# Transposes of rows in groups of eight with both evictions behind them, other places for the first weights and PSUM banks, and later row steps of the norms, in a one-core decoder layer

## The chip, the cores and the metric

The kernel runs on one core of a Trainium2 chip. The metric is the device time of one execution in microseconds (us); for the kernel before, three runs gave a median of 1337.41 us (1336.19 to 1339.85).

## The reference

One post-norm decoder layer over 1024 rows (time steps) of width 1024, all in fp32:

```
proj = h @ w_in                      # 1024 x 2824, split among three mixers
y    = concat(ssd(...), s5(...), rglru(...))            # 1024 x 1024
h = layer_norm(ALPHA*h + y @ w_out, ln1_g, ln1_b)
q, k, v = h @ wq, mem @ wk, mem @ wv                     # 256 memory rows, 4 heads
h = layer_norm(ALPHA*h + softmax(q k^T / 16) v @ wo, ln2_g, ln2_b)
h = layer_norm(ALPHA*h + square(relu(h @ w1)) @ w2, ln3_g, ln3_b)      # hidden width 4096
layer_norm(x, g, b) = (x - mean) * rsqrt(var + 1e-5) * g + b
```

The change touches what follows the mixers: the product with `w_out` and the four other large products, and the first two norms between them.

## The kernel before

**Stages.** The first 368 us compute the mixers; their result y stands transposed (channels on partitions) in SBUF. The rest is a list of eleven phases: the product with `w_out` (phase 0), with `wq` (1), with `wo` (2), and then four pairs of products with a column group of `w1` and a row group of `w2` (phases 3 to 10). Phases with an even number are called "down" (result in rows, added into the residual `acc`), those with an odd number "up" (result transposed, into the hidden tiles `h`). Attention stands between phases 1 and 2.

**Strassen steps.** Each phase multiplies 1024x1024 by 1024x1024 as 2x2 blocks of 512, by seven products of 512x512 blocks instead of eight (Strassen-Winograd). This text writes (p,s) for step s of phase p: (0,6) is the last step of phase 0, (1,0) the first of phase 1. There are 77 steps. `product` (L1242) issues one step on TensorE: 16 groups of three 128x512 matmuls (line L1255), that is 48, because each fp32 operand is held as a high part (cast to fp32r by ScalarE, L82) and a rest (VectorE, L61), tile `A`, which has one place for even and one for odd steps. Casts and splits go in halves of 128x1024, two of the four k slabs of an operand. Most steps take the groups k by k, so that the second half is first needed by the ninth group; (0,6) and (2,6) take them column by column, and need it from the third group on. A dictionary of hooks in `product` runs further code after the group of a given number.

**What stands around each step.** `prep` (L1155) makes the operands of the next step: the sums of blocks that Winograd's form asks for (`sums`, VectorE, L61) and their splits (`put`). `post` (L1262) evacuates a step's PSUM into `acc` (L79 or L61) or `h`. `load_w` (L1133) fetches a weight block in two 512 KB halves on SP's queue into one of four raw weight tiles `wr`. PSUM has two sets, used by steps in turn. TensorE's order is as written by hand; the order on the other engines is set by a scheduler at build time, which follows the order of the code where nothing else decides.

**The norms between phases.** When phase 0 or 2 finishes a block of `acc`, `measured` (L1298) takes row statistics (BN_STATS, L1302), `rstd` (L1291) joins them (BN_AGGR on VectorE, L1293), adds the epsilon on GpSimd (L1294, by the helper at L74) and raises to the power -1/2 on GpSimd (L1295, L61); `centred` (L1306) forms -mean/std on VectorE (`nmr`, L1311) and applies both on ScalarE (L1312), for four tiles of 128 rows in a block. Then `turn` (L1314) transposes the normed rows on TensorE (L1318), eight transposes of 128x128 for two 128x512 results, and evicts each result from PSUM on ScalarE with gain and bias (L1319) into `Z`, the next phase's input. Four such turns are in the last step of the down phase, (0,6) and (2,6), after groups 4, 6, 11 and 13; they turn the block that was finished first. Four more are in the first step of the up phase, (1,0) and (3,0), after groups 7, 9, 13 and 15; they turn the block finished last. `weighted` (L1336) multiplies normed rows by the gain `px` on VectorE and adds them by an accumulating DMA of GpSimd's queue to a copy of the bias in DRAM (`scr_x`), from where `fetched` (L1341) reads the residual back on SP's queue.

**The start of phase 0.** The mixers' last stores of the attention values (`scr_v`, L931) and the first loads of `w_out` into `wr` (L1141) stand in SP's queue one behind the other. During (0,0) TensorE also transposes the last four tiles of y (L951) and the norms' gains (`columns`).

## Time and profile before

| quantity | value |
|---|---|
| median of 3 runs | 1337.41 us |
| profiled execution, its own time | 1338.34 us |
| span of its trace | 1336.6 us |
| mean granted TensorE clock over the span | 0.975 |
| TensorE busy, share of the span | 95% |
| VectorE, ScalarE, GpSimd busy | 79%, 50%, 16% |

A step without any wait takes 10.9 us, at which 48 matmuls start 0.227 us apart. In the rows of the profile, PE is TensorE, DVE VectorE, ACT ScalarE, POOL GpSimd, SP the sync engine whose queue issues the loads. A row of the timeline gives start, duration, engine, line, operation, output and inputs, and in brackets the idle time before it with the engine that ended it. PEclk is the granted TensorE clock as a share of the full one.

### The profile page before, as it was taken

How to read it: one execution, taken by the hardware profiler on the slowest of the kernel's cores; microseconds unless marked ns; L12 is line 12 of the kernel's file. 1: busy time of each engine (PE TensorE's matmuls, PEld its weight loads, DVE VectorE, ACT ScalarE, POOL GpSimd, SP SyncE). 2: the span in 40 equal slices, each digit the busy share in tenths (PEclk: the TensorE clock that was granted, in tenths of full speed). 3: DMA queues.
4: the chain of work that ended last, by engine and by line, in shares of the span. 5: the costliest groups of instructions: out<-in, count | busy, mean ns of one | idle time of the engine just before them, and what ended most of it. 6: DMA issues, size and time to landing. Idle time of an engine off the chain costs nothing.

```text
span 1336.6 us, 16273 instructions
## 1 busy us (share of the span) xinstructions
PE 1266.8 (95%) x6177; PEld 1058.6 (79%) x6177; DVE 1062.3 (79%) x1431; ACT 669.9 (50%) x875; POOL 216.2 (16%) x219
## 2 busy tenths in 40 slices
PE   7979999998989879999987999999999999999996
PEld 7768777998868668898866888888888888888884
DVE  6959567368889878799777799866987699876987
ACT  6312466455443655484364573355534673355632
POOL 1614343378510210000012000000000000000004
PEclk9989999998999989999988999999999999999998
DMA  6332121345378237003816602512030201212007
GB/s 205 82 92 63 44 57 47 95 140 152 111 277 207 57 66 205 32 17 142 220 34 145 193 23 80 157 48 79 19 99 10 95 32 63 64 39 88 32 0 126
DMA packets 77550, 124.87 MB, mean 93 GB/s; under 512 B 7984, under 2 KB 42784, under 8 KB 77472
## 3 DMA queue, kind: packets, MB, share of 16 engines
q1 hardware_dynamic: 72224, 108.83, 26.3%
q0 software_dynamic: 3312, 12.06, 5.4%
q10 hardware_dynamic: 1936, 2.94, 0.6%
q8 instruction: 48, 0.79, 0.2%
q14 instruction: 30, 0.25, 0.1%
HBM read 106.87 MB, written 29.00 MB: 102 GB/s over the span
## 4 chain that ended last, share of the span: by engine, by line
PE 74%; DVE 5%; DMA 3%; ACT 3%; POOL 2%; issue 2%; SPq 0%; DVEq 0%; POOLq 0%; ACTq 0%
PE P L1255 59%; PE in L87 2%; PE in L89 2%; PE in L88 2%; DMA R<-scr_a 2%; DVE A L61 1%; PE P L1318 1%; DVE bst L1302 1%; POOL bmv L74 1%; DVE acc L61 1%; POOL bmv L61 1%; DVE wr L61 1%; ACT Z L1319 1%; PE sc L87 1%; DMA wr<-in_w_out_dram 1%
## 5 line engine op out<-in xcount | busy, mean ns | idle before, releaser
L1255 PE MATMUL P<-A 128*128 128x512 f32 x3696 | 854.7, 393 | 7.0 <-DVE A L61 3.3
L1255 PEld LDWEIGHTS P<-A 128*128 128x128 f32 x3696 | 699.0, 190 | 153.5 <-DVE A L61 4.1
L82 ACT CAST A<-wr 128x1024 fp32r<-128x1024 f32 x152 | 159.0, 1047 | 123.1 <-PE P L1255 88.5
L61 DVE TENSOR_TENSOR A<-wr,A 128x1024 fp32r<-128x1024 f32 x152 | 184.9, 1219 | 43.8 <-ACT A L82 43.7
L82 ACT CAST A<-h 128x1024 fp32r<-128x1024 f32 x88 | 92.0, 1048 | 169.1 <-PE P L1255 137.0
L74 POOL TENSOR_SCALAR bmv<-bmv 128x1 f32<-128x1 f32 x24 | 13.9, 584 | 851.5 <-DVE bmv L1293 851.5
L61 DVE TENSOR_TENSOR A<-h,A 128x1024 fp32r<-128x1024 f32 x88 | 107.2, 1222 | 42.5 <-ACT A L82 42.5
L61 DVE TENSOR_TENSOR wr<-wr,wr 128x1024 f32<-128x1024 f32 x88 | 106.4, 1220 | 22.9 <-DMA wr<-in_w_dram 19.4
L87 PE MATMUL in<-A,ring 128*128 128x512 f32 x224 | 93.1, 416 | 0.0
L89 PE MATMUL in<-A,ring 128*128 128x512 f32 x224 | 89.6, 400 | 2.3 <-POOL ring L61 2.3
L88 PE MATMUL in<-A,ring 128*128 128x512 f32 x224 | 89.2, 398 | 0.0
L61 POOL TENSOR_TENSOR ring<-raws,ring 128x512 fp32r<-128x512 f32 (+1 forms) x48 | 69.9, 1460 | 103.5 <-ACT ring L82 99.5
L82 ACT CAST A<-Z 128x1024 fp32r<-128x1024 f32 (+1 forms) x53 | 52.9, 1003 | 65.6 <-PE P L1255 52.4
L61 DVE TENSOR_TENSOR acc<-acc,P 128x1024 f32<-128x1024 f32 (+1 forms) x74 | 73.3, 1014 | 6.0 <-PE P L1255 5.3
L82 ACT CAST ring<-raws 128x512 fp32r<-128x512 f32 (+1 forms) x67 | 40.8, 616 | 63.6 <-PE in L88 22.6
L61 DVE TENSOR_TENSOR A<-Z,A 128x1024 fp32r<-128x1024 f32 (+1 forms) x53 | 61.0, 1159 | 13.1 <-ACT A L82 12.7
L89 PEld LDWEIGHTS in<-A,ring 128*128 128x128 f32 x224 | 42.7, 191 | 13.0 <-POOL ring L61 2.8
L87 PEld LDWEIGHTS in<-A,ring 128*128 128x128 f32 x224 | 43.1, 192 | 11.1 <-issue 1.8
L88 PEld LDWEIGHTS in<-A,ring 128*128 128x128 f32 x224 | 42.9, 192 | 10.8 <-issue 1.4
L1318 PE MATMUL P<-ident,acc 128*128 128x128 f32 x128 | 24.0, 312 | 24.4 <-ACT Z L1319 17.3
L1318 PEld LDWEIGHTS P<-ident,acc 128*128 128x128 f32 x128 | 16.8, 156 | 31.7 <-ACT Z L1319 21.4
L1272 ACT COPY h<-P 128x1024 f32<-128x1024 f32 x30 | 30.3, 1013 | 21.9 <-PE P L1255 21.9
(369 smaller groups left out, 1795.8 us busy)
## 6 DMA issues: line engine op xcount, KB each, us to landing
wr<-in_w_dram SPq DMA_DIRECT2D x64, 512.0 KB, 3.6
scr_x<-in_ln_dram SPq DMA_DIRECT2D x16, 512.0 KB, 13.3
scr_x<-acc POOLq DMA_DIRECT2D x16, 512.0 KB, 6.8
acc<-scr_x SPq DMA_DIRECT2D x16, 512.0 KB, 5.5
raws<-in_w_in_dram SPq DMA_DIRECT2D x28, 256.0 KB, 2.9
raws<-in_wk_dram SPq DMA_DIRECT2D x16, 256.0 KB, 3.0
R<-scr_a SPq DMA_DIRECT2D x8, 512.0 KB, 5.3
raws<-in_wv_dram SPq DMA_DIRECT2D x16, 256.0 KB, 2.9
```

Of the source, the lines that this page charges most:

```text
L61: (e or V).tensor_tensor(out=o, in0=a, in1=b, op=op)
L74: (e or V).tensor_scalar(out=o, in0=a, scalar1=s1, scalar2=None, op0=op0)
L82: ins = S.copy(out=hi, in_=src)
L87: PE.matmul(ps, lhsT=l[0], rhs=r[0], start=first, stop=False)
L88: PE.matmul(ps, lhsT=l[0], rhs=r[1], start=False, stop=False)
L89: PE.matmul(ps, lhsT=l[1], rhs=r[0], start=False, stop=last)
L1255: PE.matmul(o, lhsT=l[x_], rhs=r[y_], start=new and k == 0 and m == 0, stop=k == 3 and m == 2, skip_group_check=True)
L1272: S.copy(out=h, in_=p_)
L1302: V.bn_stats(out=st[:, t, d, :], in_=acc[:, t, d * 512:d * 512 + 512])
L1318: PE.transpose(out=ps[:, j * 128:(j + 1) * 128], in_=acc[:, b * 4 + j, k * 128:(k + 1) * 128], identity=ident)
L1319: S.activation(out=X(k // 4 + 1, b)[:, k % 4], in_=ps, func=AF.Identity, scale=lncol[:, 2 * li, k:k + 1], bias=lncol[:, 2 * li + 1, k:k + 1])
```

## The change

It has seven parts:

1. `turn` issues all eight transposes of its two results first and then the two evictions.
2. The turns stand after groups 4, 6, 8 and 10 in (0,6) and (2,6), and after 9, 11, 13 and 15 in (1,0) and (3,0).
3. The hidden tiles get their SBUF place before the raw weight tiles `wr`, and the first `w_out` blocks 11 and 12 go to `wr[0]` and `wr[1]` instead of the other way round.
4. The two PSUM sets of two tiles each are put together from the four tiles in another way.
5. `prep` of step 1 of a phase is split into two parts. At (0,0), (1,0) and (3,0) the first part is emitted ahead of the step's product, and the second part behind it; before, the whole stood behind it.
6. The epsilon is added on VectorE instead of GpSimd.
7. `weighted` is emitted at steps 2 and 3 of phases 1 and 3 instead of steps 1 and 2.

```diff
-    wrp = pool(ctx, "wraw", "right")
-    wr = [wrp.tile([128, 4, 512], F32, name=f"wr{i}") for i in range(4)]
     hp_ = pool(ctx, "hid", "right")
     H = {r: [hp_.tile([128, 4, 512], F32, name=f"h{r}{b}") for b in range(2)] for r in (1, 2)}
+    wrp = pool(ctx, "wraw", "right")
+    wr = [wrp.tile([128, 4, 512], F32, name=f"wr{i}") for i in range(4)]
...
-            PS[:] = [[pl.tile([128, 4 // n, 512], F32, tag=f"P{i}{j}", name="P") for j in range(n)] for i in range(2)]
+            t = [pl.tile([128, 4 // n, 512], F32, tag=f"P{i}", name="P") for i in range(2 * n)]
+            PS[:] = [t[:n], t[n:]] if n == 4 else [[t[3], t[1]], [t[0], t[2]]]
...
-    def prep(i):
+    def prep(i, part=None):
...
-                put(i, 0, W[12])
-                put(i, 1, B(21))
-                sums(W[21], W[21], W[22], ALU.add)
-                sums(W[11], W[21], W[11])
-                sums(sx, B(12), B(11))
-                sums(h_(22), B(22), sx)
+                if part != 2:
+                    put(i, 0, W[12])
+                    put(i, 1, B(21))
+                    sums(W[21], W[21], W[22], ALU.add)
+                    sums(W[11], W[21], W[11])
+                if part != 1:
+                    sums(sx, B(12), B(11))
+                    sums(h_(22), B(22), sx)
...
-                sums(W[21], W[21], W[22], ALU.add)
-                put(i, 0, W[21])
-                sums(sx, B(12), B(11))
-                put(i, 1, sx)
-                sums(W[11], W[21], W[11])
+                if part != 2:
+                    sums(W[21], W[21], W[22], ALU.add)
+                    put(i, 0, W[21])
+                if part != 1:
+                    sums(sx, B(12), B(11))
+                    put(i, 1, sx)
+                    sums(W[11], W[21], W[11])
...
-        ts(mv[:, 1:2], mv[:, 1:2], EPS, ALU.add, e=G)
+        ts(mv[:, 1:2], mv[:, 1:2], EPS, ALU.add)
...
         for n, k in enumerate(ks):
-            ps = P[:, n]
             for j in range(4):
-                PE.transpose(out=ps[:, j * 128:(j + 1) * 128], in_=acc[:, b * 4 + j, k * 128:(k + 1) * 128], identity=ident)
-            S.activation(out=X(k // 4 + 1, b)[:, k % 4], in_=ps, func=AF.Identity, scale=lncol[:, 2 * li, k:k + 1],
+                PE.transpose(out=P[:, n, j * 128:(j + 1) * 128], in_=acc[:, b * 4 + j, k * 128:(k + 1) * 128],
+                             identity=ident)
+        for n, k in enumerate(ks):
+            S.activation(out=X(k // 4 + 1, b)[:, k % 4], in_=P[:, n], func=AF.Identity, scale=lncol[:, 2 * li, k:k + 1],
                          bias=lncol[:, 2 * li + 1, k:k + 1])
...
-    for q, n in ((21, 3), (22, 2), (11, 1), (12, 0)):
+    for q, n in ((21, 3), (22, 2), (11, 0), (12, 1)):
...
+    prep(1, 1)
     product(0, {2: lambda: y_T(4, other[1][:, 0]), 5: lambda: y_T(5, other[0][:, 1]), 8: lambda: y_T(6, other[1][:, 1]),
                 11: lambda: y_T(7, other[0][:, 0]), 15: columns})
-    prep(1)
+    prep(1, 2)
...
-            hooks, late = turns(ph // 2, HB[ph][1], PS[(1 + ph) % 2], (4, 6, 11, 13)), True
+            hooks, late = turns(ph // 2, HB[ph][1], PS[(1 + ph) % 2], (4, 6, 8, 10)), True
...
-            hooks, late = turns(pq // 2, HB[pq][0], PS[(1 + ph) % 2], (7, 9, 13, 15)), True
+            hooks, late = turns(pq // 2, HB[pq][0], PS[(1 + ph) % 2], (9, 11, 13, 15)), True
+            prep(i + 1, 1)
...
-        if ph in (1, 3) and s_ in (1, 2):
-            weighted(ph // 2, HB[ph - 1][2 - s_])
+        if ph in (1, 3) and s_ in (2, 3):
+            weighted(ph // 2, HB[ph - 1][3 - s_])
...
         if late:
-            prep(i + 1)
+            prep(i + 1, 2 if s_ == 0 else None)
```

The lines of the changed kernel are one to eight higher than those of before: the matmuls are at L1260, the transposes at L1322, the evictions at L1325.

What TensorE runs in (0,6) around the four turns, in order; "waits" names the semaphore of the engine that the instruction waits for. Before:

```order
L1318 MATMUL P<-ident,acc 128x128 x4
L1318 MATMUL P<-ident,acc 128x128 [waits Activation_49]
L1318 MATMUL P<-ident,acc 128x128 x3
L1255 MATMUL P<-A 128x512 x6
L1318 MATMUL P<-ident,acc 128x128 [waits DVE_49]
L1318 MATMUL P<-ident,acc 128x128 x3
L1318 MATMUL P<-ident,acc 128x128 [waits Activation_49]
L1318 MATMUL P<-ident,acc 128x128 x3
L1255 MATMUL P<-A 128x512 x15
```

And in the changed kernel:

```order
L1322 MATMUL P<-ident,acc 128x128 x8
L1260 MATMUL P<-A 128x512 x6
L1322 MATMUL P<-ident,acc 128x128 x8
L1260 MATMUL P<-A 128x512 x6
L1322 MATMUL P<-ident,acc 128x128 [waits Activation_49]
L1322 MATMUL P<-ident,acc 128x128 x7
L1260 MATMUL P<-A 128x512 x6
L1322 MATMUL P<-ident,acc 128x128 [waits Activation_49]
L1322 MATMUL P<-ident,acc 128x128 x7
```

The wait between the first and the second four of each turn is gone; the third and the fourth turn wait once each, for evictions of the first and the second.

What VectorE runs from the last row steps of (0,6) into (1,0) (`acc<-acc,P` is the evacuation of (0,6)'s PSUM, `acc<-acc,px` is `weighted`, `A<-` are splits, `wr<-` sums of weights). Before:

```order
L79 SCALAR_TENSOR_TENSOR nmr<-bmv 128x1
L61 TENSOR_TENSOR acc<-acc,px 128x1024 x3
L79 SCALAR_TENSOR_TENSOR acc<-acc,P 128x2x512
L61 TENSOR_TENSOR A<-wr_3506,A 128x1024
L1302 BN_STATS bst<-acc 128x6 x2
L1293 BN_AGGR bmv<-bst 128x2
L61 TENSOR_TENSOR A<-wr_3506,A 128x1024
L79 SCALAR_TENSOR_TENSOR nmr<-bmv 128x1
L1293 BN_AGGR bmv<-bst 128x2
L61 TENSOR_TENSOR A<-Z,A 128x1024
L79 SCALAR_TENSOR_TENSOR nmr<-bmv 128x1
L61 TENSOR_TENSOR A<-Z,A 128x1024
```

And in the changed kernel:

```order
L79 SCALAR_TENSOR_TENSOR acc<-acc,P 128x2x512
L61 TENSOR_TENSOR A<-Z,A 128x1024
L1307 BN_STATS bst<-acc 128x6 x2
L1298 BN_AGGR bmv<-bst 128x2
L61 TENSOR_TENSOR A<-wr_3512,A 128x1024
L74 TENSOR_SCALAR bmv<-bmv 128x1
L1298 BN_AGGR bmv<-bst 128x2
L61 TENSOR_TENSOR A<-wr_3512,A 128x1024
L79 SCALAR_TENSOR_TENSOR nmr<-bmv 128x1
L74 TENSOR_SCALAR bmv<-bmv 128x1
L61 TENSOR_TENSOR A<-Z,A 128x1024
L79 SCALAR_TENSOR_TENSOR nmr<-bmv 128x1
```

`weighted` no longer stands ahead of the evacuation, the epsilon additions (L74) are in VectorE's row, and between the evacuation and the last `nmr` there are four splits of 128x1024 where there were three.

What SP's queue holds at the start of phase 0. Before:

```order
L931 DMA scr_v<-kv 128x256 x2
L1141 DMA wr_3508<-in_w_out_dram 128x2x512
L931 DMA scr_v<-kv 128x256 x2
L1141 DMA wr_3508<-in_w_out_dram 128x2x512
L1141 DMA wr_3507<-in_w_out_dram 128x2x512 x2
L1433 DMA px<-in_ln_dram 48x128
L1141 DMA wr_3506<-in_w_out_dram 128x2x512 x2
```

And in the changed kernel:

```order
L931 DMA scr_v<-kv 128x256 x4
L1142 DMA wr_3515<-in_w_out_dram 128x2x512 x2
L1142 DMA wr_3514<-in_w_out_dram 128x2x512 x2
L1439 DMA px<-in_ln_dram 48x128
L1142 DMA wr_3512<-in_w_out_dram 128x2x512 x2
```

The first half of the first weight block stood ahead of the last two stores and now stands behind them.

More of the change, by code (lines that the diff above doesn't have):

```diff
@@ L1080 @@
     acc = pool(accst, "acc", "left").tile([128, 8, D], F32, name="acc")
+    hp_ = pool(ctx, "hid", "right")
+    H = {r: [hp_.tile([128, 4, 512], F32, name=f"h{r}{b}") for b in range(2)] for r in (1, 2)}
     wrp = pool(ctx, "wraw", "right")
     wr = [wrp.tile([128, 4, 512], F32, name=f"wr{i}") for i in range(4)]
-    hp_ = pool(ctx, "hid", "right")
-    H = {r: [hp_.tile([128, 4, 512], F32, name=f"h{r}{b}") for b in range(2)] for r in (1, 2)}
     PS = []
```

## The prediction

> **What bounds the kernel now.** I read the page first, for the bounding engine:
>
> ```profile
> PE 1266.8 (95%) x6177; PEld 1058.6 (79%) x6177; DVE 1062.3 (79%) x1431; ACT 669.9 (50%) x875; POOL 216.2 (16%) x219
> L1318 PE MATMUL P<-ident,acc 128*128 128x128 f32 x128 | 24.0, 312 | 24.4 <-ACT Z L1319 17.3
> ```
>
> TensorE is busy for 95% of the span, and the largest single idle time that the change touches stands ahead of the norm transposes: 24.4 us, as much as the transposes themselves take. The waits of TensorE split it by what ended it:
>
> ```profile
> PE P L1318 <- ACT Z L1319: 17.3, 16, 3.3
> PE P L1318 <- ACT acc L1312: 7.0, 4, 2.0
> ```
>
> Sixteen waits for the eviction ScalarE makes between the two fours of a turn, and four for normed rows. Then the windows show each step's price. The columns are the stretch, its length, each engine's busy time with its instructions, the granted clock, the DMA share and GB/s. The stretches are the steps (0,6), (1,0), (1,1), (2,6), (3,0), and all steps after 790 us:
>
> ```profile
> 442.30:465.70 23.40, 17.28 (x81) 13.38 (x80) 21.42 (x26) 13.76 (x16) 5.10 (x6) 0.93 0.04 5
> 465.70:492.80 27.10, 19.80 (x81) 15.35 (x81) 17.32 (x20) 14.06 (x16) 4.95 (x6) 0.81 0.41 75
> 492.80:503.70 10.90, 10.90 (x49) 9.01 (x48) 10.90 (x11) 5.22 (x6) 3.46 (x4) 1.00 0.49 73
> 676.00:699.50 23.50, 17.60 (x81) 13.97 (x80) 18.44 (x23) 13.60 (x15) 3.35 (x6) 0.88 0.06 8
> 699.50:724.80 25.30, 18.60 (x82) 14.35 (x81) 17.41 (x20) 13.15 (x15) 4.96 (x6) 0.84 0.69 160
> 790.00:1323.00 533.00, 533.00 (x2354) 441.43 (x2352) 443.16 (x410) 261.32 (x264) 10.14 (x17) 1.00 0.20 61
> ```
>
> An undisturbed step is (1,1): 10.9 us, or 0.227 us for each of 48 matmuls. After 790 us 49 such steps fill 533 us, with TensorE never idle, so nothing can be won there. The four norm steps take 23.4, 27.1, 23.5 and 25.3 us: 99.3 us where four undisturbed ones take 43.6. This is what the change acts on.
>
> **The change part by part. Grouping in eights, later places, in (0,6) and (2,6).** TensorE's timeline in (0,6), at the second four of its first and of its last turn, and at those of the last turn in (2,6) (start, duration, then the idle time before it in brackets):
>
> ```profile
> 446.01 1.19 PE L1255 MATMUL P<-A 128*128 128x512 f32 x4 [1.66 <-DVE A L61]
> 448.51 0.66 PE L1318 MATMUL P<-ident,acc 128*128 128x128 f32 x4 [0.87 <-ACT Z L1319]
> 448.93 1.64 PE L1255 MATMUL P<-A 128*128 128x512 f32 x6
> 461.59 0.87 PE L1318 MATMUL P<-ident,acc 128*128 128x128 f32 x4 [1.85 <-ACT Z L1319]
> 694.75 1.12 PE L1318 MATMUL P<-ident,acc 128*128 128x128 f32 x4 [3.29 <-ACT Z L1319]
> ```
>
> The last four of a turn end and the next matmul starts 448.93-448.51 = 0.42 us behind their start, so eight transposes cost about 0.9 us (an estimate). The 0.87 us wait goes, since the evictions come after the eighth. They need not end before the next matmuls, which write another PSUM set; the third turn needs the first one's tile, two groups of six matmuls (2.7 us) and a turn (0.9 us) later, while two evictions take 1.5 us. The 1.85 and 3.29 us arise because ScalarE runs a norm step ahead of the eviction; in the changed order all evictions of (0,6) stand ahead of the next norm steps. What is late next in (0,6) is the 1.66 us wait for VectorE's split `A`, which no part removes; one more small instruction and a reordered split ahead of it make it about 2.3 (bounds 1.7 and 2.9, one 128x1024 operation more). So (0,6) is 10.9 + 4x0.9 + 2.3 = 16.8, which is 6.6 less than 23.4; the clock, 0.93 before, I put at full, as no gap of TensorE stays over 2.3 us. In (2,6) no split is waited for: 10.9 + 3.6 = 14.5, 9.0 less than 23.5.
>
> **Grouping, later places, the split `prep` and the epsilon, in (1,0) and (3,0).** Here the turns wait for the rows, and VectorE, GpSimd and ScalarE form a chain:
>
> ```profile
> 465.95 1.22 DVE L79 SCALAR_TENSOR_TENSOR acc<-acc,P 128x1024 f32<-128x1024 f32 x1 [0.49 <-PE P L1255]
> 467.09 1.22 DVE L61 TENSOR_TENSOR A<-wr,A 128x1024 fp32r<-128x1024 f32 x1
> 468.22 1.28 DVE L1302 BATCH_NORM_STATS2 bst<-acc 128x6 f32<-128x512 f32 x2
> 469.42 0.19 DVE L1293 BATCH_NORM_AGGREGATE bmv<-bst 128x2 f32<-128x12 f32 x1
> 469.78 1.00 POOL L74 TENSOR_SCALAR bmv<-bmv 128x1 f32<-128x1 f32 x1 [3.17 <-DVE bmv L1293]
> 470.86 0.57 POOL L61 TENSOR_TENSOR bmv<-bmv,nhalf 128x1 f32<-128x1 f32 x1
> 471.47 0.16 DVE L79 SCALAR_TENSOR_TENSOR nmr<-bmv 128x1 f32<-128x1 f32 x1 [0.77 <-POOL bmv L61]
> 473.79 1.24 ACT L1312 ACTIVATE acc<-acc,nmr,bmv 128x1024 f32<-128x1024 f32 x1 [0.89 <-DVE nmr L79]
> ```
>
> A VectorE operation of 128x1024 follows the last after 1.14 us (465.95 to 467.09). Call E the end of (0,6), 465.7 before. The evacuation started at E+0.25 and the last norm step ended at 475.03, E+9.3. The epsilon on GpSimd cost 1.00 us, on VectorE (0.1 us, the step of 469.42) it is cheap, but it now queues behind splits. What of that chain shortens is paid for otherwise: (0,6) is 6.6 us shorter, and VectorE, busy 21.4 of its 23.4 us, has row work left at E. From the last split needed in (0,6), 4.6 us before E, it has 6.0 us of statistics, weight sums and `nmr` to do (three 128x1024, two pairs of statistics, the waits for GpSimd), so the evacuation starts at E+1.5. Then follow the rows of the changed order: evacuation, split, two statistics, split, split at 1.14 each (1.2 for the statistics), small ones 0.3: 6.1 us, and the power, which ends about 0.4 after a VectorE operation that runs beside it:
>
> ```profile
> 1326.14 1.42 DVE L79 SCALAR_TENSOR_TENSOR acc<-acc,bmv,sx 128x512 f32<-128x512 f32 x2
> 1327.06 0.93 POOL L61 TENSOR_TENSOR bmv<-bmv,nhalf 128x1 f32<-128x1 f32 x1
> ```
>
> (1327.99 against 1327.56, where it took 0.93 instead of 0.57). Thus the first `nmr` is at E+8.0; a split, and the power again, the second at E+9.7; its norm step, 1.2 us, ends at E+10.9. The Trainium skill, "GPSIMD Engine Reference", section 1, lists SBUF interfaces shared with VectorE; these two rows agree.
>
> ```profile
> 470.55 0.38 PE L1318 MATMUL P<-ident,acc 128*128 128x128 f32 x2
> 475.09 0.33 PE L1318 MATMUL P<-ident,acc 128*128 128x128 f32 x1 [1.80 <-ACT acc L1312]
> 476.28 1.11 PE L1318 MATMUL P<-ident,acc 128*128 128x128 f32 x4 [0.87 <-ACT Z L1319]
> 477.05 2.91 PE L1255 MATMUL P<-A 128*128 128x512 f32 x6
> ```
>
> Before, TensorE came to its first turn at 470.55 after 21 matmuls, E+4.9. Now it comes after 27, E+6.1, and waits 4.8 us for the last row tile. Behind that stand the turn's last four or five transposes, 0.5, then 21 matmuls, 4.8, and three turns, 2.7: 10.9+8.0 = 18.9, 19.0 rounded, at full clock. At 477.05 six matmuls took 2.91 us instead of 1.64: the clock was at half. The stretches of half clock in these steps, each 3.41 us:
>
> ```profile
> 475.55:478.96 3.41, 2.68 (x9) 2.29 (x10) 3.41 (x4) 2.13 (x3) 0.95 (x1) 0.50 0.41 43
> 478.96:482.37 3.41, 2.54 (x10) 1.84 (x9) 1.65 (x2) 1.15 (x2) 0.00 (x0) 0.50 0.57 111
> 482.37:485.78 3.41, 3.41 (x11) 2.73 (x10) 1.23 (x1) 0.78 (x1) 0.00 (x0) 0.50 0.00 0
> 707.65:711.06 3.41, 1.30 (x6) 1.02 (x6) 3.41 (x4) 1.96 (x2) 1.82 (x2) 0.50 0.69 175
> 711.06:714.47 3.41, 3.41 (x12) 2.61 (x10) 3.31 (x3) 1.82 (x2) 0.00 (x0) 0.50 1.07 174
> ```
>
> TensorE worked 2.68+2.54+3.41 = 8.6 us at half clock in (1,0), a loss of 4.3, and 1.30+3.41 = 4.7 in (3,0), a loss of 2.4. The waits that bring it on stay, so I keep both losses; the bounds are none, and all 8.0 us behind the wait at half clock. (1,0) is 19.0+4.3 = 23.3, 3.8 less than 27.1. In (3,0) a gain multiplication stands in the chain as well; replayed in the same way its last norm step ends at E+12.5, so 12.5+8.0+2.4 = 22.9, 2.4 less than 25.3.
>
> **First weights.** SP's queue at the start, and who waits for it:
>
> ```profile
> 367.11 0.38 SPq L1141 DMA_DIRECT2D wr<-in_w_out_dram  x1
> 368.61 0.80 SPq L931 DMA_DIRECT2D scr_v<-kv  x2
> 386.65 5.52 PE L1255 MATMUL P<-A 128*128 128x512 f32 x16 [1.59 <-DVE A L61]
> ```
>
> The first half block now stands behind the stores that wait until 368.61, and issues near 369.5 instead of 367.11; all weights behind it move too. The sums for (0,1) need the block after it, and TensorE waited for their split at 386.65. I add 1.3 us: between 0 (the loads share the same bandwidth and end no later) and 2.4 (the whole shift).
>
> **Parts at nothing.** The other PSUM tiles only rename what is waited for, and are covered by the 3.6 us between a turn and the next use of its tile. The gain multiplications and their DMAs move to (1,1) to (1,3), where VectorE was full for 10.9 us but TensorE never waited; the splits it needs stand ahead of them. The tail's epsilon changes by under 0.5 us either way, as the power there already runs beside VectorE.
>
> **Sum.** -6.6-9.0-3.8-2.4+1.3 = -20.5, from the profiled execution's 1338.3: 1317.8. The median of the runs shown is 0.9 lower than that execution, so 1317.
>
> **The rivals.** *The clock.* The Trainium skill, "TensorE: Matmul & The Clock Gate", Part 4, says of transposes that the full clock "doesn't engage" for them, because they don't count as busy in the same way. As a mechanism of this kernel: at half clock six matmuls take 2.9 us and eight transposes 1.8 to 2.2, in turns, so no stretch of 3.41 us is filled with matmuls; and 475.55 to 478.96, with 1.9 us of matmuls, did not end the half clock, while 711.06 to 714.47, with some 2.6, did. If it stays down to the end of the turns, (1,0) is 27.0 and (3,0) 28.5, together 9.3 more than my sum: 1326. For: the row of 475.55. Against: that of 711.06. I give 0.22.
>
> *The row chain is no shorter.* GpSimd's power is held up by the splits on VectorE, which now run in denser order, or ScalarE's norm steps queue behind casts; then (1,0) and (3,0) gain nothing: -14.3, 1323. For: (1,0)'s chain is already 1.6 us longer in my replay, relative to E. I give 0.12.
>
> *The chain is freer.* The clock recovers at once and the first weights come no later: 6.7 and 1.3 less, 1309. For: the 1.00 us that an epsilon cost. I give 0.12.
>
> *Slower: SP's queue in phase 3.* With the multiplications a step later, their accumulating DMAs are later, and the reads of `scr_x` that wait for them stand on SP's queue ahead of the second `w2` blocks.
>
> ```profile
> scr_x<-acc POOLq DMA_DIRECT2D x16, 512.0 KB, 6.8
> acc<-scr_x SPq DMA_DIRECT2D x16, 512.0 KB, 5.5
> wr<-in_w_dram SPq DMA_DIRECT2D x64, 512.0 KB, 3.6
> ```
>
> In my replay the weights arrive about 1 us ahead of the sum that (3,4) needs. Each us beyond that costs one, and it decides the sign from 21.5 us of delay on (20.5 and the 1 us), more than one whole pass through the three transfers (15.9); two passes, 31.8 us, would give 1317+31 = 1348. Against: one such pass is what the median transfers take, and they run side by side. I give 0.02. That the change does not do what it says is excluded by the orders: the wait between the fours is gone.
>
> **How the numbers follow.** Forecast 1317, chance 0.5, its own range 1312 to 1321 by the bounds of the split (0.6 each way), the first weights (1.3) and some of the clock. Clock 0.22 at 1326, chain 0.12 at 1323, freer 0.12 at 1309, slower 0.02 at 1348, and 0.02 for several of these losses together, about 1335. The range 1308 to 1327 takes in all but these last two and the tails of the others. 0.3% is 4 us, about what a measurement of this kernel can tell from no change. The slower case lies above that band, and the several losses together reach into it, with a part of the slower case that falls short: faster 0.95, same 0.03, slower 0.02.
>
> **What would show each step.** Right: in the changed profile the idle time ahead of the transposes falls from 24.4 to under 12 us, with no wait for evictions; (0,6) and (2,6) take 16 to 17 and 14 to 15 us; the first turn of (1,0) waits 4 to 6 us for normed rows; half-clock stretches remain in (1,0) and (3,0) only. Wrong: (1,0) or (3,0) above 25 us with a clock below 0.8 would be the clock, above 25 with a late norm step the chain; (0,1) as long as before says that the first weights were not late; a wait for `A` or for `wr` in (1,1) to (3,4) is the queue.

## The result and the profile after

The changed kernel takes 1320.40 us (median of 4 runs, 1319.09 to 1322.26) against 1338.13 us (median of 4) of the kernel before: a ratio of 0.9869, 95% interval 0.985 to 0.9888. The profiled execution took 1319.8 us, with a span of 1318.0. In the profile after, the page's row of busy times:

```profile
PE 1261.5 (96%) x6177; PEld 1057.2 (80%) x6177; DVE 1063.9 (81%) x1455; ACT 667.3 (51%) x875; POOL 216.7 (16%) x195
```

and the norm transposes among the groups of instructions (busy time, mean ns of one, idle time ahead and what ended it):

```profile
L1322 PE MATMUL P<-ident,acc 128*128 128x128 f32 x128 | 20.3, 304 | 9.6 <-ACT acc L1317 9.6
```

The idle time ahead of the transposes fell from 24.4 to 9.6 us. The waits of TensorE say what is left of it, and show two that were not there before:

```profile
PE P L1322 <- ACT acc L1317: 9.6, 4, 3.8
PE P L1445 <- DVE Z L61: 2.2, 1, 2.2
PE P L1260 <- ACT h L1419: 0.7, 1, 0.7
```

No wait for an eviction remains; four waits for normed rows do, two in (1,0) and two in (3,0). The two new ones are the second, ahead of the gains' transpose in (0,0), and the third, in the attention stage. The windows of the changed kernel, in order: (0,0) and (0,1) together, (0,6), (1,0), (2,6), (3,0), and the tail behind the last matmul:

```profile
366.90:400.90 34.00, 28.62 (x116) 21.46 (x115) 28.11 (x30) 11.88 (x17) 4.07 (x6) 0.85 0.72 271
444.40:461.40 17.00, 14.76 (x81) 12.22 (x80) 16.40 (x23) 10.67 (x14) 1.49 (x2) 1.00 0.00 1
461.40:483.30 21.90, 17.54 (x81) 14.58 (x80) 18.96 (x25) 14.19 (x16) 7.88 (x7) 0.84 0.38 63
667.50:681.90 14.40, 14.40 (x81) 12.29 (x80) 14.40 (x19) 10.06 (x13) 0.47 (x1) 1.00 0.01 2
681.90:704.90 23.00, 17.73 (x81) 14.75 (x80) 18.74 (x27) 14.09 (x16) 8.29 (x8) 0.85 0.64 130
1303.50:1318.00 14.50, 0.07 (x1) 0.00 (x0) 6.01 (x12) 2.30 (x2) 4.67 (x6) 0.64 0.70 146
```

And the kernel before in the two stretches of these that were not shown of it, (0,0) with (0,1), and the tail:

```profile
368.60:398.80 30.20, 26.42 (x113) 20.74 (x114) 26.39 (x28) 10.33 (x12) 2.62 (x4) 0.94 0.80 304
1323.30:1336.60 13.30, 0.05 (x1) 0.00 (x0) 5.55 (x9) 2.30 (x2) 4.26 (x7) 0.58 0.85 158
```

The four norm steps went from 99.3 to 76.3 us, 23.0 less. The span is 18.6 us shorter, so 4.4 us were given back: 2.0 at the start (measured from the last `kv` matmul, which ends at 367.0 us in the trace of before and at 367.1 in that of after, to the end of (0,1) at 398.8 and 400.8), 1.2 in the tail, and 0.9 in the attention stage between (1,6) and (2,0), which took 53.4 instead of 52.5 us; the rest is rounding. TensorE's timeline at the first turn of (0,6) shows the new form of a turn:

```profile
448.58 1.20 PE L1260 MATMUL P<-A 128*128 128x512 f32 x4 [2.24 <-DVE A L61]
449.62 1.04 PE L1322 MATMUL P<-ident,acc 128*128 128x128 f32 x8
450.41 1.64 PE L1260 MATMUL P<-A 128*128 128x512 f32 x6
```

The matmuls start 450.41-449.62 = 0.79 us behind the first of the eight transposes, with no wait between. Four turns lengthen (2,6) by 14.45-10.88 = 3.57 us, so a whole turn costs 0.9. What waits is the split `A` ahead of the turn. In (1,0), the timelines of VectorE, GpSimd and TensorE:

```profile
462.88 1.22 DVE L79 SCALAR_TENSOR_TENSOR acc<-acc,P 128x1024 f32<-128x1024 f32 x1
469.33 0.16 DVE L79 SCALAR_TENSOR_TENSOR nmr<-bmv 128x1 f32<-128x1 f32 x1 [0.44 <-POOL bmv L61]
469.47 1.22 DVE L61 TENSOR_TENSOR A<-Z,A 128x1024 fp32r<-128x1024 f32 x1
471.13 0.16 DVE L79 SCALAR_TENSOR_TENSOR nmr<-bmv 128x1 f32<-128x1 f32 x1 [0.44 <-POOL bmv L61]
```

```profile
469.70 1.39 POOL L61 TENSOR_TENSOR bmv<-bmv,nhalf 128x1 f32<-128x1 f32 x1 [0.40 <-DVE bmv L74]
```

```profile
470.82 0.33 PE L1322 MATMUL P<-ident,acc 128*128 128x128 f32 x1 [2.89 <-ACT acc L1317]
472.62 1.33 PE L1322 MATMUL P<-ident,acc 128*128 128x128 f32 x5 [1.47 <-ACT acc L1317]
473.59 2.91 PE L1260 MATMUL P<-A 128*128 128x512 f32 x6
477.86 1.79 PE L1260 MATMUL P<-A 128*128 128x512 f32 x6
```

The step starts at E = 461.4. The evacuation starts at E+1.5, the two last `nmr` come at E+7.9 and E+9.7, and the power on GpSimd (1.39 us, the second row) ends 0.40 us behind the split that runs beside it on VectorE (471.09 against 470.69). TensorE waits 2.89 and 1.47 us; the first six matmuls behind that run at half clock, and from 477.86 the clock is nearly back at full.

### The profile page after: what moved, and what is told of

It is laid out like the page before. It is cut to its first block, busy times and chain, and to the rows that moved or that the text cites. A ratio compares the mean times of both kernels' runs of the same rounds, so it can differ in the third digit from the quotient of the medians.

```text
span 1318.0 us, 16260 instructions
## 1 busy us (share of the span) xinstructions
PE 1261.5 (96%) x6177; PEld 1057.2 (80%) x6177; DVE 1063.9 (81%) x1455; ACT 667.3 (51%) x875; POOL 216.7 (16%) x195
## 5 line engine op out<-in xcount | busy, mean ns | idle before, releaser
L1260 PE MATMUL P<-A 128*128 128x512 f32 x3696 | 851.6, 392 | 5.9 <-DVE A L61 3.3
L1260 PEld LDWEIGHTS P<-A 128*128 128x128 f32 x3696 | 696.1, 189 | 152.2 <-DVE A L61 5.0
L61 POOL TENSOR_TENSOR bmv<-bmv,nhalf 128x1 f32<-128x1 f32 x24 | 30.0, 1252 | 826.1 <-DVE bmv L74 716.8
L82 ACT CAST ring<-raws 128x512 fp32r<-128x512 f32 (+1 forms) x67 | 40.8, 616 | 63.7 <-PE in L88 22.4
L87 PEld LDWEIGHTS in<-A,ring 128*128 128x128 f32 x224 | 43.0, 192 | 11.2 <-issue 1.8
L1277 ACT COPY h<-P 128x1024 f32<-128x1024 f32 x30 | 30.4, 1013 | 24.3 <-PE P L1260 24.3
L61 DVE TENSOR_TENSOR A<-sx,A 128x1024 fp32r<-128x1024 f32 x32 | 38.9, 1223 | 1.9 <-ACT A L82 1.9
L89 PE MATMUL z<-ring,A 128*128 128x260 f32 x128 | 37.7, 294 | 1.7 <-DVE A L61 1.7
## 6 DMA issues: line engine op xcount, KB each, us to landing
scr_x<-in_ln_dram SPq DMA_DIRECT2D x16, 512.0 KB, 12.4
```

Of the source, the lines that this page charges most:

```text
L61: (e or V).tensor_tensor(out=o, in0=a, in1=b, op=op)
L82: ins = S.copy(out=hi, in_=src)
L87: PE.matmul(ps, lhsT=l[0], rhs=r[0], start=first, stop=False)
L89: PE.matmul(ps, lhsT=l[1], rhs=r[0], start=False, stop=last)
L1260: PE.matmul(o, lhsT=l[x_], rhs=r[y_], start=new and k == 0 and m == 0, stop=k == 3 and m == 2, skip_group_check=True)
L1277: S.copy(out=h, in_=p_)
```

## The experiments

The theories are named by letters, which the expectations use. A says that the waits for evictions were the cost, and part 1 alone removes them. Its rival B says that the later places and row steps make the gain. C to F are about the epsilon and the start, G and H about the clock, I about parts 3 to 7 together, J, M and N about what bounds (1,0) and (3,0) next. Where a diff below leaves lines out, "..." stands for them.

**Part 1 alone, on the kernel before.** The edit is the `turn` of the diff above, nothing else.

> The kernel before with part 1 alone (eight transposes, then the two evictions). Theory A, that the waits for evictions are the main cost and the grouping takes them away: (0,6) 16 to 18 us, (2,6) 14 to 15.5, (1,0) and (3,0) 23 to 26; in all about 1322 (1319 to 1326), more than 80% of the whole gain. Theory B, that the later places of the turns and the later row steps make the gain, and the grouping alone only moves the wait to the rows: not below 1330.

Measured: 1319.89 us, ratio 0.9876 (0.9856 to 0.9896), the whole of the changed kernel's gain. The windows (0,6), (1,0), (2,6), (3,0) of this kernel:

```profile
444.70:461.10 16.40, 14.72 (x81) 12.20 (x80) 15.65 (x21) 10.18 (x14) 1.62 (x3) 1.00 0.00 1
461.10:485.40 24.30, 17.97 (x82) 14.85 (x81) 19.97 (x24) 15.07 (x17) 8.40 (x10) 0.79 0.51 85
668.50:683.00 14.50, 14.50 (x82) 12.34 (x81) 14.44 (x17) 8.84 (x11) 0.99 (x1) 1.00 0.01 2
683.00:707.90 24.90, 17.34 (x82) 14.27 (x81) 19.30 (x25) 15.35 (x17) 8.87 (x12) 0.79 0.71 151
```

(0,6) and (2,6) are already where the changed kernel has them; (1,0) and (3,0) are 2.4 and 1.9 us longer than there. Theory A holds. It does not lose in total, as it also lacks the losses of the other parts: in its profile the start is 0.6 us, the tail 1.5 and the attention stage 0.8 shorter than in the changed kernel's.

**All parts but part 1.** The eviction goes back into the loop over the two results:

```diff
         for n, k in enumerate(ks):
+            ps = P[:, n]
             for j in range(4):
...
-        for n, k in enumerate(ks):
-            S.activation(out=X(k // 4 + 1, b)[:, k % 4], in_=P[:, n], func=AF.Identity, scale=lncol[:, 2 * li, k:k + 1],
+            S.activation(out=X(k // 4 + 1, b)[:, k % 4], in_=ps, func=AF.Identity, scale=lncol[:, 2 * li, k:k + 1],
```

> The changed kernel with the eviction put back behind each four transposes, all else as changed. Theory A: the 0.87 us wait is back 4 times in each of four steps, and (0,6) and (2,6) are some 3.5 to 5 us longer, (1,0) and (3,0) 3 to 4 and what the clock adds: 1333 to 1339. Theory B: at most 1327.

Measured: 1337.49 us (median of 10), ratio 1.0009 (0.9993 to 1.0025): no gain in total. Its waits for evictions were back, sixteen of them:

```profile
PE P L1323 <- ACT Z L1324: 13.9, 16, 0.9
PE P L1323 <- ACT acc L1317: 8.5, 4, 3.2
```

For the total this settles A against B: part 1 is enough for the gain, and without it there is none. B's mechanism exists all the same. In this profile (0,6), (1,0), (2,6) and (3,0) took 21.4, 25.8, 18.9 and 25.3 us, 91.4 together and 7.9 less than before, as no wait for an eviction was longer than 0.9 us, where the longest had been 3.3. What the other parts gain there they give back elsewhere, 4.4 us of it at the start (2.4), in the tail (1.2) and in the attention stage (0.8); the profiled execution, 1335.56 us, was also the fastest of the ten.

**Old places of the turns.** Part 2 undone:

```diff
-            hooks, late = turns(ph // 2, HB[ph][1], PS[(1 + ph) % 2], (4, 6, 8, 10)), True
+            hooks, late = turns(ph // 2, HB[ph][1], PS[(1 + ph) % 2], (4, 6, 11, 13)), True
...
-            hooks, late = turns(pq // 2, HB[pq][0], PS[(1 + ph) % 2], (9, 11, 13, 15)), True
+            hooks, late = turns(pq // 2, HB[pq][0], PS[(1 + ph) % 2], (7, 9, 13, 15)), True
```

> The changed kernel with the turns at their old places (groups 4, 6, 11, 13 and 7, 9, 13, 15). Theory A: nothing in (0,6) and (2,6); in (1,0) and (3,0) the first turn is reached two groups (1.4 us) earlier and waits that much longer, with 27 instead of 21 matmuls behind it, 1.4 us more each, up to 3 with the clock: 1321 to 1326. Theory B: 1328 or more.

Measured: 1323.50 us, ratio 0.9907 (0.9889 to 0.9924). (0,6) and (2,6) took 17.0 and 14.5 us as in the changed kernel, (1,0) 23.4 and (3,0) 23.8, which is 1.5 and 0.8 more. So the later places are worth about 2.3 us in the steps, less than the 2.8 that the two groups give if the clock is the same.

**The epsilon back on GpSimd.** Part 6 undone:

```diff
-        ts(mv[:, 1:2], mv[:, 1:2], EPS, ALU.add)
+        ts(mv[:, 1:2], mv[:, 1:2], EPS, ALU.add, e=G)
```

> The changed kernel with the epsilon back on GpSimd. Theory C, that a GpSimd step beside a VectorE operation ends some 0.1 to 0.4 us behind it whichever it is, so that moving the epsilon only hands the long step from the epsilon (1.00 us) to the power (1.4 us): (1,0) and (3,0) within 1 us of the changed kernel's 21.9 and 23.0, and the tail behind the last matmul 1 us shorter, as before: 1318 to 1321. Theory D, that the epsilon on VectorE shortened the row chain by about 1 us a row, two rows in each of (1,0) and (3,0): 3 to 5 us longer, 1323 to 1325.

Measured: 1320.49 us, ratio 0.988 (0.9862 to 0.9899), the same as the change; (1,0) 22.6 and (3,0) 23.2 us, 0.9 more together; (0,6) 16.4 us, 0.6 less; the attention stage 0.6 more; the tail 12.7 us instead of 14.5. GpSimd's groups of epsilon and power in this kernel, then the power's in the changed one (busy time, then mean ns of one):

```profile
L74 POOL TENSOR_SCALAR bmv<-bmv 128x1 f32<-128x1 f32 x24 | 15.5, 649 | 824.8 <-DVE bmv L1298 824.8
L61 POOL TENSOR_TENSOR bmv<-bmv,nhalf 128x1 f32<-128x1 f32 x24 | 13.8, 577 | 1.7
```

```profile
L61 POOL TENSOR_TENSOR bmv<-bmv,nhalf 128x1 f32<-128x1 f32 x24 | 30.0, 1252 | 826.1 <-DVE bmv L74 716.8 <-DVE bmv L1298 109.3
```

Epsilon and power took 649+577 = 1226 ns on GpSimd; with the epsilon on VectorE the power alone took 1252. Theory C holds: in the rows of (1,0) and (3,0), whichever GpSimd step comes first ends behind the VectorE operation beside it. In the tail the moved epsilon costs: 14.0 to 15.0 us in the six profiles with it on VectorE, 12.2 to 13.3 in the eight with it on GpSimd. But the total of this run is the same, so part 6 as a whole is not shown to cost anything. GpSimd's queue in the tail, before and after:

```profile
1321.86 0.56 POOL L61 TENSOR_TENSOR bmv<-bmv,nhalf 128x1 f32<-128x1 f32 x1
1322.38 0.93 POOL L1363 DMA_DIRECT2D out_dram<-acc  x1
```

```profile
1302.38 1.45 POOL L61 TENSOR_TENSOR bmv<-bmv,nhalf 128x1 f32<-128x1 f32 x1 [0.38 <-DVE bmv L74]
1303.80 0.88 POOL L1369 DMA_DIRECT2D out_dram<-acc  x1
```

The last engine work of the tail ends 6.1 us behind the last matmul before and 6.0 after, so the last rows are not later. What is later is the store of an earlier row tile, which stands in GpSimd's queue behind a power: it is issued 0.2 us behind the end of the last matmul (1303.6) where it was 1.0 ahead of it (1323.4). That this delay of 1.2 us is the whole loss of the tail is likely, but no run shows it alone.

**The start, in two runs.** First `prep(1)` whole behind the product of (0,0), then the old weight places:

```diff
-    prep(1, 1)
...
-    prep(1, 2)
+    prep(1)
```

> The changed kernel with prep(1) emitted whole behind (0,0)'s product, as before. In the changed kernel (0,0) and (0,1) together take 33.9 us, 3.7 more than before, of which 1.7 is an earlier start. Theory E, that the weight blocks come late and VectorE's sums wait for them: within 0.5 us of 33.9, since the same sums wait for the same loads, though the 2.25 us wait ahead of the gains' transpose moves. Theory F, that the earlier sums and splits on VectorE hold up the evacuation which that transpose waits for: about 2 us less, 31.5 to 32.3.

```diff
-    hp_ = pool(ctx, "hid", "right")
-    H = {r: [hp_.tile([128, 4, 512], F32, name=f"h{r}{b}") for b in range(2)] for r in (1, 2)}
     wrp = pool(ctx, "wraw", "right")
     wr = [wrp.tile([128, 4, 512], F32, name=f"wr{i}") for i in range(4)]
+    hp_ = pool(ctx, "hid", "right")
+    H = {r: [hp_.tile([128, 4, 512], F32, name=f"h{r}{b}") for b in range(2)] for r in (1, 2)}
...
-    for q, n in ((21, 3), (22, 2), (11, 0), (12, 1)):
+    for q, n in ((21, 3), (22, 2), (11, 1), (12, 0)):
```

> The changed kernel with the weight tiles and the first blocks at their old places (part 3 undone), the new banks and the split prep kept. Theory E: the first half block issues about 3 us earlier, the sums on VectorE no longer wait for a load, and (0,0) and (0,1) take 31.0 to 32.5 together instead of 33.9; in all 1.5 to 3 us less, 1317.5 to 1319. Theory F: 33.5 to 34.3, and 1320 to 1321.

Measured: 1320.88 us, ratio 0.9879 (0.9864 to 0.9894), with 33.5 us for (0,0) and (0,1), for the first; 1318.14 us, ratio 0.986 (0.9845 to 0.9875), with 31.8 us, for the second. Theory E holds. SP's queue and VectorE in the changed kernel:

```profile
370.44 1.96 SPq L1142 DMA_DIRECT2D wr<-in_w_out_dram  x4
377.77 1.23 DVE L61 TENSOR_TENSOR wr<-wr,wr 128x1024 f32<-128x1024 f32 x1 [2.39 <-DMA wr<-in_w_out_dram]
```

and with the old weight places:

```profile
367.80 0.38 SPq L1142 DMA_DIRECT2D wr<-in_w_out_dram  x1
376.50 2.57 DVE L61 TENSOR_TENSOR wr<-wr,wr 128x1024 f32<-128x1024 f32 x2 [0.46 <-DMA wr<-in_w_out_dram]
```

The first load issues 2.6 us earlier, and VectorE waits 0.46 instead of 2.39 us for the weights. The new 2.25 us wait ahead of the gains' transpose costs nothing by itself: with `prep(1)` whole it was 0.87 us, the wait behind it grew from 1.81 to 3.44, and the time stayed.

**Work in the wait.** Extra matmuls, whose results are overwritten, ahead of the third and fourth transpose of the first turn of (1,0) and of (3,0):

```diff
-    def turn(li, b, ks, P):
+    FILL = (10, 5)
+
+    def turn(li, b, ks, P, fill=None):
         for n, k in enumerate(ks):
             for j in range(4):
+                if fill and n == 0 and j > 1:
+                    for m in range(FILL[j - 2]):
+                        PE.matmul(P[:, 1], lhsT=fill[0][:, 0, 0:128], rhs=fill[1][:, 0], start=True, stop=True,
+                                  skip_group_check=True)
...
-            hooks, late = turns(pq // 2, HB[pq][0], PS[(1 + ph) % 2], (9, 11, 13, 15)), True
+            hooks, late = turns(pq // 2, HB[pq][0], PS[(1 + ph) % 2], (9, 11, 13, 15),
+                                (slot(i, 0)[0], slot(i, 1)[0])), True
```

> The changed kernel with 10 and 5 extra matmuls ahead of the third and the fourth transpose of the first turn of (1,0) and (3,0), into the turn's second bank, which is overwritten afterwards: work that is not needed, put where TensorE waits for normed rows. Theory G, that the clock falls because TensorE stands idle there, and holds through the turns once it is up: no half clock in (1,0) and (3,0), which take 19.0 to 20.0 and 20.0 to 21.0 us instead of 21.9 and 23.0: 1315 to 1316.5. Theory H, that stretches of turns with 60% matmuls are themselves too little, or that the extra matmuls delay the rows' transposes: a half clock comes later in the turns all the same, and less than 2 us is won: 1318.5 to 1320.5.

Measured: 1315.13 us, ratio 0.9836 (0.9818 to 0.9854). The windows of (1,0) and (3,0):

```profile
462.30:481.50 19.20, 18.30 (x96) 14.88 (x95) 17.88 (x24) 14.04 (x16) 7.85 (x7) 1.00 0.35 55
680.10:700.30 20.20, 18.38 (x96) 14.88 (x96) 18.67 (x27) 14.03 (x16) 8.27 (x8) 1.00 0.66 131
```

The clock is 1.00 in both, and they are 2.7 and 2.8 us shorter, with the rows as late as in the changed kernel (E+11.1 and E+12.1). Theory G holds: the half clock came from the idle wait, and the mixture of six matmuls and eight transposes does not bring it on.

**Parts 1 and 2 alone.** Parts 3 to 7 of the diff above are undone.

> The kernel before with parts 1 and 2 alone (grouping and later places); parts 3 to 7 undone. Theory A, that these two carry the gain, and the rest costs at the start and at the tail: (0,6) and (2,6) 16.5 and 14.5, (1,0) and (3,0) 22 to 23.3, (0,0) and (0,1) together 30 to 31.7, the tail 12.7 to 13.4; 1316 to 1318.5. Theory I, that parts 3 to 7 gain as well: 1321 or more.

Measured: 1316.18 us, ratio 0.9844 (0.9828 to 0.986). (0,6) 16.5, (1,0) 22.4, (2,6) 14.5, (3,0) 23.9 us; (0,0) with (0,1) 30.4, the attention stage 52.6, the tail 12.4. The gain of the two parts is all there, and the three losses are gone. The attention stage took 53.4 to 54.1 us in the seven profiles with the new banks and 52.5 to 52.6 in six of the seven with the old; the seventh (55.6) had a half clock in that stage. The 0.7 us wait for `h` quoted above is part of it. The banks also have a gain: all seven profiles with the old ones have this wait ahead of (0,0), here of before, and none with the new ones has it:

```profile
368.64 1.66 PE L1255 MATMUL P<-A 128*128 128x512 f32 x6 [1.60 <-ACT kv L930]
```

It buys no time, since (0,1) waits for its split in any case: with the new banks and the old weight places it ended 31.6 us behind the last `kv` matmul, with both old 31.3 to 33.2. No run changed the banks alone. Part 5 at (1,0) and (3,0) moves no row in the order of any engine, so it does nothing there; parts 4 and 7 were not undone one at a time, and their own shares stay open.

**Rows first.** On the kernel with parts 1 and 2, the splits and sums for (1,1) and (3,1) and the gain multiplications are ordered on VectorE behind the last `nmr` (`issue_after` adds this order, `nmr_` holds the last `nmr` instruction):

```diff
-            weighted(ph // 2, HB[ph - 1][2 - s_])
+            with tc.issue_after(nmr_[0]):
+                weighted(ph // 2, HB[ph - 1][2 - s_])
...
-        if late:
+        if late and s_ == 0:
+            with tc.issue_after(nmr_[0]):
+                prep(i + 1)
+        elif late:
             prep(i + 1)
```

> The kernel before with parts 1 and 2, and with the splits and sums for (1,1) and (3,1) and the gain multiplications ordered behind the last nmr on VectorE. Theory J, that the splits standing between the row steps are what the first turn of (1,0) and (3,0) waits for: the evacuation starts 0.3 us behind the end of the step ahead, the last norm step ends 6 to 7 us behind it, the first turn waits under 1.5 us, (1,0) and (3,0) take 14.6 to 16.5 us instead of 22.4 and 23.9, without a half clock; 1299 to 1304. Theory M, that VectorE has no room for it: what is moved back makes TensorE wait for A in (1,1) to (1,3) and (3,1) to (3,3), and more than half is given back; 1308 or more.

Measured: 1314.65 us, ratio 0.9834 (0.9812 to 0.9856). J was right about the two steps and M about the total: (1,0) took 15.4 and (3,0) 15.4 us at full clock, and (1,3) and (1,4) 18.0 and 14.4 instead of 10.9 each; another 3.4 us went between (3,1) and (3,6). ScalarE and TensorE in (1,3) and (1,4):

```profile
509.23 1.05 ACT L82 CAST VV<-px 128x1024 fp32r<-128x1024 f32 x1 [10.99 <-DMA scr_x<-acc]
515.06 0.80 PE L1259 MATMUL P<-A 128*128 128x512 f32 x1 [5.05 <-ACT A L82]
```

ScalarE stood 11 us at the cast into `VV`, a tile of the attention that takes over memory of `acc`; the row names the accumulating DMAs, which read `acc`, as what it waited for (directly then, and not by way of `px`, as the expectation of a later run puts it). The casts for the next steps were queued behind it. M had expected waits for VectorE's splits; the long one, 5.05 us, was for ScalarE's cast.

**The split first.** In addition, the evacuation of (0,5) behind the last split for (0,6), which `last_sub` holds:

```diff
-        if i != 14:
+        if i == 6:
+            with tc.issue_after(last_sub[0]):
+                post(i - 1)
+        elif i != 14:
             post(i - 1)
```

> The kernel of the run with the rows first, and with the evacuation of (0,5) ordered behind the last split that (0,6) needs. If the 2.1 us wait of (0,6) is that split queued behind an evacuation of 128x1024: (0,6) takes 14.5 to 15.5 us instead of 16.5, and the whole 1 to 2 us less than that run. If the split waits for its cast on ScalarE anyway, or the turns then wait for the evacuation: (0,6) stays at 16 us or more.

Measured: 1314.03 us, ratio 0.983 (0.9812 to 0.9848). (0,6) took 14.5 us without a wait for `A`; it was 16.5 with parts 1 and 2 alone and had fallen to 15.4, with a wait of 0.52, in the run before. So what was left of the wait, 0.9 us of the step, was that split queued behind an evacuation; for the rest this run is no test. (1,0) became 1 us longer, and the total is the same within the interval.

**Gain multiplications not held, at steps 2 and 3.**

```diff
-        if ph in (1, 3) and s_ in (1, 2):
-            with tc.issue_after(nmr_[0]):
-                weighted(ph // 2, HB[ph - 1][2 - s_])
+        if ph in (1, 3) and s_ in (2, 3):
+            weighted(ph // 2, HB[ph - 1][3 - s_])
```

> The kernel of the run with the split first, but with the gain multiplications no longer held behind the last nmr, and emitted at steps 2 and 3 (part 7). In the two runs before it, ScalarE stood 11 us at the cast of VV in (1,3), which waits by way of px for the last of the accumulating DMAs, and the casts for (1,3) and (1,4) were queued behind it. Theory N, that this is what gave the gain back: with the multiplications spread as in the changed kernel, (1,3) and (1,4) go back to 10.9 us each, (1,0) and (3,0) take 16.5 to 18.5 us because some multiplications stand in the row chain again, (0,6) stays at 14.5: 1305 to 1309. Theory M, that VectorE is simply full there: the waits for A stay in (1,2) to (1,4) in another form, and the time stays above 1311.

Measured: 1312.34 us, ratio 0.9814 (0.9783 to 0.9845): above the 1311 of M, but not by M's mechanism, as no wait for `A` stayed in (1,2) to (1,4). (1,3) and (1,4) went back to 10.9 us, as N said, but the multiplications in the row chain cost more than N expected: (1,0) 21.2 us with its half clock back, (3,0) 18.6. The profiled execution also had the half clock in the attention stage named above, 3 us.

**Held, at steps 2 and 3.**

```diff
-            weighted(ph // 2, HB[ph - 1][3 - s_])
+            with tc.issue_after(nmr_[0]):
+                weighted(ph // 2, HB[ph - 1][3 - s_])
```

> The kernel of the run before (gain multiplications at steps 2 and 3), but with them held behind the last nmr again, so that none stands in the row chain; ScalarE's cast of VV now stands behind all casts for (1,4). Theory N, that the row chain and the cast of VV are two separate costs: (1,0) and (3,0) 15.3 to 16.5 us without a half clock, as in the two runs with the multiplications held, and (1,3) and (1,4) 10.9 us each; 1303 to 1308. Theory M, that VectorE has no room for both: waits for A or for the cast of VV come back between (1,1) and (1,6) or (3,1) and (3,4), more than 6 us of them, and the time is 1310 or more.

Measured: 1309.78 us, ratio 0.9792 (0.9764 to 0.9819), the fastest of all, 10.6 us below the changed kernel. The windows (1,0), (1,4) and (3,0), VectorE in phase 3, and TensorE there:

```profile
458.20:474.60 16.40, 14.89 (x81) 12.32 (x80) 14.29 (x18) 14.32 (x16) 1.98 (x5) 1.00 0.00 0
507.60:522.50 14.90, 12.78 (x50) 10.09 (x49) 8.47 (x9) 4.36 (x5) 0.15 (x1) 0.89 1.05 275
676.60:691.90 15.30, 14.82 (x81) 12.11 (x79) 13.48 (x17) 12.17 (x15) 1.54 (x4) 1.00 0.01 1
```

```profile
720.01 4.61 DVE L61 TENSOR_TENSOR acc<-acc,px 128x1024 f32<-128x1024 f32 x4
724.55 2.35 DVE L85 TENSOR_TENSOR A<-wr,A 128x1024 fp32r<-128x1024 f32 x2
```

```profile
728.09 32.29 PE L1261 MATMUL P<-A 128*128 128x512 f32 x134 [2.10 <-DVE A L85]
```

N holds for the two steps and for (1,3), but four multiplications in one block (4.6 us) now stand ahead of the splits for (1,4) and for (3,4): a wait of 2.1 us in each, and with the half clock that follows 4.0 us each. These two waits cost more than the 1.8 us by which N's range was missed; spreading the four multiplications was not tried.

## Why the prediction was right

It forecast 1317 (1308 to 1327), faster; the median is 1320.4. The mechanism, sixteen waits that go with the grouping, is confirmed, but the closeness of the number owes something to luck: (1,0) gained 1.4 us more than its term, while the start, the tail and the attention stage cost 2.8 us more than theirs. By its steps:

- (0,6) and (2,6): 6.6 and 9.0 us were forecast, 6.4 and 9.0 measured (23.4 to 17.0, 23.48 to 14.45). The step that the 0.87 us waits go with the grouping is the one that the runs with and without part 1 confirm. The remaining wait for `A` was 2.24 us, put at 2.3. That (0,6) kept its full clock was forecast because no gap stays over 2.3 us. It came true, but the reason is no rule: in the last run gaps of 2.1 us were followed by half clock.
- The chain in (1,0): the evacuation at E+1.5, `nmr` at E+8.0 and E+9.7 and the last norm step at E+10.9 were forecast; they came at E+1.5, E+7.9, E+9.7 and E+11.2. The first turn waited 4.4 us where 4.8 were forecast. In (3,0) the last norm step ended at E+12.1, forecast E+12.5.
- The clock: 4.3 us of loss were kept for (1,0), from three stretches of half clock. There were two, and TensorE worked 5.6 us in them, a loss of 2.8; this is the term that was mis-sized, and (1,0) fell by 5.2 instead of 3.8. In (3,0) it worked 6.1 us, a loss of 3.0 where 2.4 were kept; the rows came 0.4 earlier than forecast, and the step fell by 2.3 (forecast 2.4). The run with work in the wait gives about the same prices, 2.7 and 2.8. The stretches of half clock of the changed kernel between the mixers and the tail, the first of them in (0,0) and (0,1):

```profile
382.63:392.87 10.24, 7.32 (x17) 4.76 (x17) 10.24 (x11) 4.18 (x4) 0.00 (x0) 0.50 1.03 418
471.38:478.20 6.82, 5.58 (x20) 4.90 (x21) 6.73 (x6) 2.63 (x3) 2.79 (x3) 0.50 0.42 61
693.24:700.07 6.83, 6.06 (x21) 5.28 (x22) 6.25 (x6) 2.59 (x4) 2.61 (x3) 0.50 0.70 113
```

- The rival by which the half clock lasts through the turns did not come about: at 477.86 six matmuls took 1.79 us, with two turns to go. The Trainium skill, "TensorE: Matmul & The Clock Gate", Part 4, has it that transposes do not engage the full clock; here (2,6), with 32 transposes among its matmuls, ran at 1.00, and so did (1,0) and (3,0) once the wait was filled. No run has a stretch of transposes alone.
- The first weights: 1.3 us, of 0 to 2.4; measured 2.0. The delay itself was sized right. The load issued at 370.44, some 0.9 later than put, and TensorE's wait for the split of (0,1) ended at 387.99 instead of 386.65, 1.3 later:

```profile
387.99 14.39 PE L1260 MATMUL P<-A 128*128 128x512 f32 x52 [1.11 <-DVE A L61]
```

- The other 0.7 of the start is the clock behind that wait, which stayed at half until 392.87 where it had been at half from 386.80 to 390.21. That half clock would remain in (1,0) and (3,0) only was forecast, and was wrong here. The run with the old weight places confirms the cause of the delay. The size varies from profile to profile: from the last `kv` matmul to the end of (0,1) it was 31.3 to 33.2 us in the eight with the old places, 33.3 to 34.2 in the six with the new.
- Parts at nothing: this step failed in two terms. The tail's epsilon was put at under 0.5 us either way, since the power runs beside VectorE before as after; the tail is 1.2 longer. The reason rested on the one row of 1327.06. Of the eight powers of the last norm the other seven took 0.56 or 0.57 us before; after, all eight took 0.92 to 1.46, with the late store shown above. And the banks were put as covered by the turns, with no look at the attention stage, which is 0.9 us longer. These two and 0.7 at the start, less the 1.4 of (1,0), make most of the 2.0 us by which the profiled execution (1319.8) is above the sum (1317.8). The rest of the difference lies in the median: before it was 0.9 below the profiled execution, after 0.6 above.
- The rival of a slower outcome, loads behind `scr_x` in phase 3: no step between (3,1) and (3,6) was longer than 10.91 us.

The forecast put the reason for the gain into parts 1, 2, 5 and 6 together. The runs are sharper: part 1 carries it, part 2 adds 2 to 4 us, and parts 3 to 7 together take 3 to 4 us back (1316.18 us without them). Of these, part 3 takes about 2 us (1318.14 with the old weight places); part 6 lengthens the tail, but with it undone the total is the same; and 0.9 us in the attention stage goes with the new banks of part 4, which no run changed alone.

## What to carry to other kernels

When an engine alternates short work with an eviction that it then waits for, do the work of two buffers first and evict both behind it: here it took away sixteen waits of 0.87 us or more, 17.3 us in all. Look at each part of a bundled change for what it costs elsewhere, the start and the tail above all; here 4 of 23 us were given back outside the steps that the change was made for. When such a wait is gone, the next one is in the order of the helper engine, and work moved out of its way must be followed to its last consumer, as with the cast of `VV`.

## What the runs showed of the hardware

A one-column step on GpSimd that ran beside a 128x1024 split or sum of VectorE ended a fixed time behind it: the epsilon 0.08 us (it took 1.00 us at 469.78 in the kernel before, 0.21 without such an operation beside it), the power 0.41 us (1.39 at 469.70 in the changed kernel, 0.56 without). Not every operation holds it: beside row statistics the power took 0.55 us (at 437.88 in the changed kernel), and beside evacuations, which read PSUM, 0.57 (at 1312.63 in the kernel before). An idle time of TensorE of 2.1 us was followed by a whole 3.41 us stretch at half clock (510.71 to 514.13) in (1,4) of the last run, so that it cost 4.0 us; one of 2.24 us in (0,6) of the changed kernel was followed by none. Thirty matmuls whose results are not used made the kernel 5 us faster: with them the clock was 1.00 in both steps instead of 0.84 and 0.85.
